# Dilated attention heads: tokens ordered by their rest by 4, 384 score columns per softmax row

## The chip, the cores and the metric

The kernel runs on one core of a Trainium2 chip, as one program from its inputs in DRAM to its output. The metric is the device time of one execution in microseconds (us); the tables give the median of several runs. The profile is of one execution of its own.

## The reference, cut to what matters

256 tokens of width 1024 go through two blocks of two layers each. The change lies in the second block, whose layers (`hybrid_layer`) have three branches: a short convolution, a latent attention and the dilated attention. In the dilated branch 8 heads of 64 look at the tokens in three groups, each with its own q, k and v:

```python
DIL_PATTERNS = ((128, 1), (512, 4), (2048, 16))   # window, dilation
for gi, (window, dilation) in enumerate(DIL_PATTERNS):
    o_g, lse_g = dilated_group_attention(dq[:, :, gi], dk[:, :, gi], dv[:, :, gi], slopes[gi],
                                         dilation, window // dilation)
alpha = jax.nn.softmax(jnp.stack(lses, axis=0), axis=0)
o_c = jnp.sum(alpha[..., None] * jnp.stack(outs, axis=0), axis=0)
```

Group 0 looks back over up to 128 tokens one by one. Group 1 looks at tokens a multiple of 4 back, group 2 at tokens a multiple of 16 back, causally, each with a bias that falls with the distance. So in groups 1 and 2 a token sees only tokens with its own rest by 4. The last two lines make one softmax of the three groups: a row of scores over all three, one maximum, one sum.

## The kernel before, in words

**Weights.** A load on SyncE's DMA queue (SP) brings 1 MB of weights into a tile `raw` (L328, two buffers and now and then a third). ScalarE (ACT) casts each half to `whi` (L350), VectorE (DVE) forms the rest `wlo` (L351). Each plain matmul of 512 columns (`mm`, L280) takes one of these against the activations `hT`. `tr` (L284) transposes a 128×128 block on TensorE (PE).

**Order.** On PE the order is written out: jobs are Python generators that say after how many microseconds they want to go on (`yield D_DQ`, `yield D_SOFTD`), and each emitted matmul moves the planner's clock by the time written beside it. The other engines' queues are ordered by the framework's scheduler, which looks at the program and at when inputs are expected.

**The dilated branch.** `dilated()` projects q, k and v in nine blocks of four units (one unit: a pair of heads, one of q, k, v, one group; 128 columns), for two token tiles t of 128. The epilogue `epi` normalizes q and k (`rows`, L1495), transposes them and copies them to `dq` (ACT, L1510) and `dk` (DVE, L1512). v units are copied from PSUM by ACT to `dvn` (L1500, two buffers) and moved by SP's DMAs to `dv` (L1502; all three tiles are called `dqkv` in the profile), since there the tokens change partitions. Each v run has two DMAs per token tile, of 64 rows and of 1 to 3 units of 512 bytes. Tokens are ordered by their rest by 2: the even ones are one tile, the odd ones the other. For comparison with these DMAs: L1307 loads `gc`, 64 rows of 4 bytes, and L629 loads `acc`, one row of 4 KB, both on SP too.

**One pair.** `dil_pair()` runs once a pair of heads (4 pairs in each of 2 layers), when the blocks with its q, k and v are done. It loads two bias tables `dtab` (L1532), then for each tile t and head (rows 0 to 63 or 64 to 127 of the array) makes four score matmuls of 128×128: two for group 0 (own tile and the other), one each for groups 1 and 2 (own tile: even distances contain the multiples of 4 and 16, the table masks the rest). DVE adds the table and takes the maximum (L1549), ACT takes exp with the sum (L1552), DVE the reciprocal (L1553), ACT scales the row (L1554): all on 128×512, called `dsm`. After D_SOFTD the four blocks of each `dsm` are transposed on PE and copied by ACT to `daT` (L1560), and 16 matmuls with 64 columns of `dv` as weights (PV) collect the output, which ACT copies to `ocT` (L1568).

Of the kernel before, what the change touches and what calls it, by code (L numbers as in the profile page):

```python
# [10 lines left out]
F32 = mybir.dt.float32  # L11
F32R = mybir.dt.float32r
AF = mybir.ActivationFunctionType
ALU = mybir.AluOpType
# [7 lines left out]
NEG = -1e30  # L22
BIG = 1e30
WB = 8
AT0, DSM, DAT, GT = 8, 4, 4, 2
# [114 lines left out]
def constants():  # L140
    f = np.float32
    o = {}
    i = np.arange(128)
# [25 lines left out]
    n = 24  # L169
    m = 2.0 ** (-8.0 * np.arange(1, n + 1) / n).reshape(3, 8)  # L170


    tab = np.zeros((8, 128, 5, 128))
    for c, (gi, off) in enumerate(((0, -1), (0, 0), (1, 0), (2, 0), (0, 1))):
        dl = (1, 4, 16)[gi]
        dist = 2 * (i[:, None] - i[None, :]) + off
        ok = (dist >= 0) & (dist % dl == 0) & (dist // dl <= 128)
        for h in range(8):
            tab[h, :, c] = np.where(ok, -m[gi, h] * dist * 8.0, NEG)
    o["k_dil"] = tab.reshape(8, 128, 640).astype(f)  # L180
    return o


# [49 lines left out]

DIL_COLS = [[(0, 1), (0, 0), (1, 0), (2, 0)], [(0, 1), (1, 1), (2, 1), (0, 0)]]


class Job:
# [6 lines left out]
class Kern:  # L246
# [1216 lines left out]
    def dilated(self, q, gqk, ocT):  # L1463
        V, A, wk = self.V, self.A, self.wk
        pj, jobs, bufs = [], {}, {}
        eo = lambda x, g, n, t: x.rearrange("p g (r t i) -> p g t r i", r=2, t=2)[:, g:g + n, t]

        def buf(p, s):
            if (p, s) not in bufs:
                bufs[p, s] = q.tile([128, 2, 384] if s == 2 else [128, 3, 256], F32, tag=("dq", "dk", "dv")[s], bufs=2,  # L1470
                                    name=self.nm("dqkv"))
            return bufs[p, s]

        def epi(b, t, _, ps):
# [29 lines left out]
            tp = self.trs(rows, nu).rearrange("p g (i r) -> p g r i", r=2)  # L1504
            for i, (p, s), g, n in runs:
                if s == 2:
                    continue
                part = tp[:, i - u0:i - u0 + n]
                if s == 0:
                    A.copy(eo(buf(p, 0), g, n, t), part)  # L1510
                else:
                    V.tensor_tensor(eo(buf(p, 1), g, n, t), part,  # L1512
                                    gqk[:, g:g + n, None, None].to_broadcast([128, n, 2, 64]), ALU.mult)
# [10 lines left out]
    def dil_pair(self, pr, dq, dk, dv, ocT, deps):  # L1524
# [3 lines left out]
        V, A = self.V, self.A  # L1528
        tabs = []
        for j in range(2):  # L1530
            tab = self.ph.tile([128, 640], F32, tag="dtab", bufs=2, name=self.nm("dtab"))
# [6 lines left out]
        for t in range(2):  # L1538
            for o in (0, 64):
                ps[t, o] = self.bank()  # L1540
            for i, (g, k) in enumerate(DIL_COLS[t]):
                for o in (0, 64):
                    self.mm(ps[t, o][:, i * 128:i * 128 + 128], dq[o:o + 64, g, t * 128:t * 128 + 128],
                            dk[o:o + 64, g, k * 128:k * 128 + 128], us=0.12)
        for t in range(2):
            for o in (0, 64):
                st = self.wk.tile([128, 6], F32, tag="st", bufs=8, name=self.nm("dst"))
                sm = self.ph.tile([128, 512], F32, tag="dsm", bufs=DSM, name=self.nm("dsm"))
                V.tensor_tensor_reduce(sm, ps[t, o], tabs[o // 64][:, t * 128:t * 128 + 512], 1.0, NEG, ALU.add, ALU.max,  # L1549
                                       st[:, 0:1])  # L1550
                V.tensor_scalar_mul(st[:, 2:3], st[:, 0:1], -0.125)
                A.activation(sm, sm, AF.Exp, bias=st[:, 2:3], scale=0.125, accum_out=st[:, 3:4])  # L1552
                V.reciprocal(st[:, 3:4], st[:, 3:4])  # L1553
                A.activation(sm, sm, AF.Copy, scale=st[:, 3:4])  # L1554
                sms[t, o] = sm
        yield D_SOFTD
        for t in range(2):
            for o in (0, 64):
                aTs[t, o] = self.ph.tile([128, 4, 128], F32, tag="daT", bufs=DAT, name=self.nm("daT"))
# [8 lines left out]
        A.copy(ocT[:, pr].rearrange("p (n r) -> p r n", r=2), pv[:, :256].rearrange("p (r n) -> p r n", r=2))  # L1568


def build(tc, a, stop=99):
# [66 lines left out]
```

## Time and profile before

| what | value |
|---|---|
| median of 3 runs | 1474.86 us (1474.18 to 1477.39) |
| the profiled execution, its own time | 1475.15 us |
| its span | 1473.2 us |
| PE, DVE, ACT busy, share of the span | 98%, 73%, 56% |
| dilated stretch of layer 0, of layer 1 | 880 to 1030 us, 1240 to 1390 us |

The span is what the profiler saw between the first and the last instruction; 1.95 us of the execution lie outside it. Lines of the timeline give the start, the length and the operation, with the output tile, the inputs and the shape; neighbours of one kind are drawn together with their count. Matmul records overlap, so their pace is the difference of starts. A matmul in 32-bit floats (scores, PV) has two records, a transpose or a plain matmul has one. On SP the length is that of the issue, not of the transfer. A window's line gives its ends and length, then the busy time of PE, of PE's weight loads, of DVE, ACT and POOL, each with its instructions, then the granted clock of PE, the DMA share and the GB/s.

### The profile page before, as it was taken

The page shows a single profiled execution, that of the slowest core. Times are in us where ns is not written, and L with a number is a line of the kernel's source. Part 1 is how long each engine was busy: PE and PEld are TensorE (multiplying, and loading weights), DVE is VectorE, ACT ScalarE, POOL GpSimd, SP SyncE. Part 2 cuts the span into 40 slices and gives each one's busy share as a digit, 9 for nine tenths or more (in the row PEclk, how much of TensorE's full clock was granted, in tenths as well). Part 3 has the DMA queues.
Part 4 walks back from the last instruction along what each step waited for, and adds up shares of the span by engine and source line. Part 5 has one row for each costly group of instructions (what it writes and reads, how often), then busy time and mean ns, then how long its engine had stood idle before and what let it go on. Part 6 is the DMA issues. An engine that isn't in the chain of part 4 may idle for free. (4 is left out here: it accounts for less than half of the span.)

```text
span 1473.2 us, 20311 instructions
## 1 busy us (share of the span) xinstructions
PE 1448.1 (98%) x7636; PEld 1193.5 (81%) x7636; DVE 1070.6 (73%) x1779; ACT 817.7 (56%) x1417; POOL 109.9 (7%) x88
## 2 busy tenths in 40 slices
PE   9999999999999999999999999999999999999998
PEld 6776788888887888888878788888888888888887
DVE  5698898956999848866378766666767976665674
ACT  4657556634534535665265754667445675566651
POOL 0000100000001100000022003120001101221000
PEclk9999999999999999999999999999999999999999
DMA  9757587765867638745444355544545535554542
GB/s 380 281 200 272 200 318 282 286 215 179 304 246 269 235 138 273 270 172 202 159 145 172 116 207 211 185 167 159 198 163 200 203 116 206 200 178 173 186 178 79
DMA packets 53093, 306.53 MB, mean 208 GB/s; under 512 B 7674, under 2 KB 12154, under 8 KB 20100
## 3 DMA queue, kind: packets, MB, share of 16 engines
q1 hardware_dynamic: 51988, 304.74, 57.5%
q8 instruction: 60, 0.98, 0.3%
q10 hardware_dynamic: 1008, 0.50, 0.1%
q14 instruction: 37, 0.30, 0.1%
HBM read 301.03 MB, written 1.05 MB: 205 GB/s over the span
## 5 line engine op out<-in xcount | busy, mean ns | idle before, releaser
L351 DVE TENSOR_TENSOR wlo<-raw,whi 128x1024 fp32r<-128x1024 f32 x448 | 533.9, 1214 | 128.5 <-ACT whi L350 126.9
L350 ACT CAST whi<-raw 128x1024 fp32r<-128x1024 f32 x450 | 458.7, 1044 | 235.9 <-PE p L280 176.9
L280 PE MATMUL p<-whi,hT 128*128 128x512 f32 (+1 forms) x1728 | 573.7, 400 | 1.1 <-ACT whi L350 0.5
L280 PEld LDWEIGHTS p<-whi,hT 128*128 128x128 f32 x1728 | 325.4, 189 | 74.3 <-issue 6.9
L280 PE MATMUL p<-hT,whi 128*128 128x512 f32 x1088 | 382.9, 402 | 0.0
L280 PE MATMUL p<-wlo,hT 128*128 128x512 f32 (+1 forms) x864 | 337.3, 390 | 1.5 <-DVE wlo L351 1.5
L280 PE MATMUL p<-hT,wlo 128*128 128x256 f32 x1088 | 286.5, 283 | 0.0
L280 PEld LDWEIGHTS p<-hT,whi 128*128 128x128 f32 x1088 | 198.0, 190 | 37.8 <-issue 0.7
L280 PEld LDWEIGHTS p<-hT,wlo 128*128 128x128 f32 x1088 | 206.9, 190 | 12.3
L280 PEld LDWEIGHTS p<-wlo,hT 128*128 128x128 f32 x864 | 163.5, 189 | 34.0 <-DVE wlo L351 2.7
L637 DVE SCALAR_TENSOR_TENSOR acc<-raw,csc,acc 128x1024 f32<-128x1024 f32 x80 | 102.2, 1278 | 4.4 <-DMA raw<-in_ada_w_dram 4.0
L514 POOL TENSOR_TENSOR dss<-dss,mh 128x8 f32<-128x8 f32 (+3 forms) x36 | 56.1, 1560 | 328.0 <-DVE dss L513 328.0
L280 PE MATMUL p<-whi,ah 128*128 128x512 f32 x176 | 69.7, 396 | 0.0
L280 PE MATMUL p<-whi,al 128*128 128x512 f32 x176 | 69.5, 395 | 0.0
L280 PE MATMUL p<-wlo,ah 128*128 128x512 f32 x176 | 69.5, 395 | 0.0
L1495 DVE TENSOR_TENSOR rows<-p,dss 128x512 f32<-128x512 f32 (+3 forms) x36 | 18.5, 514 | 46.2 <-POOL dss L514 46.2
L1018 ACT COPY fT<-p 128x256 f32<-128x256 f32 x72 | 26.1, 368 | 42.7 <-PE p L280 42.5
L280 PE MATMUL p<-whi,s 128*128 128x512 f32 x128 | 41.3, 397 | 0.0
L280 PEld LDWEIGHTS p<-whi,al 128*128 128x128 f32 x176 | 33.0, 187 | 8.1
L280 PEld LDWEIGHTS p<-wlo,ah 128*128 128x128 f32 x176 | 33.0, 187 | 7.9
L280 PEld LDWEIGHTS p<-whi,ah 128*128 128x128 f32 x176 | 33.0, 187 | 7.9
L280 PE MATMUL p<-whi,yh 128*128 128x512 f32 x96 | 38.4, 400 | 0.0
(278 smaller groups left out, 1628.3 us busy)
## 6 DMA issues: line engine op xcount, KB each, us to landing
raw<-in_w_in_dram SPq DMA_DIRECT2D x84, 1024.0 KB, 4.9
raw<-in_w_gu_dram SPq DMA_DIRECT2D x44, 1024.0 KB, 5.3
raw<-in_ada_w_dram SPq DMA_DIRECT2D x40, 1024.0 KB, 5.3
raw<-in_w_ret_dram SPq DMA_DIRECT2D x24, 1024.0 KB, 6.0
raw<-in_w_dn_dram SPq DMA_DIRECT2D x22, 1024.0 KB, 4.9
raw<-in_w_qkv_dram SPq DMA_DIRECT2D x11, 1024.0 KB, 10.0
as<-in_ada_s_dram SPq DMA_DIRECT2D x16, 512.0 KB, 8.8
raw<-in_w_ro_dram SPq DMA_DIRECT2D x8, 1024.0 KB, 5.2
```

Of the source, the lines that this page charges most:

```text
L280: self.T.matmul(out, lhsT=lhsT, rhs=rhs, start=first, stop=last, skip_group_check=skip)
L350: for ins in (self.A.copy(hi[:, :m * n], src), self.sub.tensor_tensor(lo[:, :m * n], src, hi[:, :m * n].bitcast(F32), ALU.subtract)):
L351: self.sub.tensor_tensor(lo[:, :m * n], src, hi[:, :m * n].bitcast(F32), ALU.subtract)):
L514: self.G.tensor_tensor(ss, ss, self.mh[:, :n], ALU.pow)
L637: self.V.scalar_tensor_tensor(acc, r[:, j * D:j * D + D], self.sc[:, k:k + 1], acc, ALU.mult, ALU.add)
L1018: A.copy(f, ps[:, 256:512])
L1495: V.tensor_tensor(d3(rows[:, :nu * 128]), d3(src), ss[:, :2 * nu, None].to_broadcast([128, 2 * nu, 64]), ALU.mult)
```

## The change

Tokens are ordered by their rest by 4: tile t holds the tokens with rests 2t and 2t+1, 64 each. A group 1 or 2 score block of one rest is now 64×64, and both groups' blocks share one block of 128 columns. A softmax row has 384 columns: two blocks for group 0, one for groups 1 and 2.

- Scores: 16 matmuls of 128×128 become 8 of 128×128 and 16 of 64×64.
- Transposes: 16 become 12. `dsm`, `daT` and the operations on them have 384 columns, the table 512 where it had 640.
- PV: 16 matmuls of 64×128 become 8 of 64×128 and 8 of 64×64.
- `dv` has six blocks of 128 columns: 0 and 1 for group 0, four (one a rest) for groups 1 and 2, whose keys share the 128 rows. The DMAs per token tile and v run were 2 (64 rows) and are 4 times the run's units (32 rows of 512 bytes): 24 a layer before, 96 after.

```diff
-DIL_COLS = [[(0, 1), (0, 0), (1, 0), (2, 0)], [(0, 1), (1, 1), (2, 1), (0, 0)]]
+DIL_COLS = [[1, 0, None], [1, None, 0]]
...
-        eo = lambda x, g, n, t: x.rearrange("p g (r t i) -> p g t r i", r=2, t=2)[:, g:g + n, t]
+        eo = lambda x, g, n, t: x.rearrange("p g (r t i) -> p g t r i", r=4, t=2)[:, g:g + n, t]
...
-                bufs[p, s] = q.tile([128, 2, 384] if s == 2 else [128, 3, 256], F32, tag=("dq", "dk", "dv")[s], bufs=2,
+                bufs[p, s] = q.tile([128, 6, 128] if s == 2 else [128, 3, 256], F32, tag=("dq", "dk", "dv")[s], bufs=2,
...
-                    for r in range(2):
-                        self.nc.sync.dma_start(buf(p, 2)[64 * t:64 * t + 64, r, cs(g, n)], nat[r:128:2, :n * 128])
+                    for r in range(4):
+                        for u in range(n):
+                            at, c = (64 * (r % 2), r // 2) if g + u == 0 else (64 * (g + u - 1), 2 + r)
+                            self.nc.sync.dma_start(buf(p, 2)[at + 32 * t:at + 32 * t + 32, c], nat[r:128:4, cs(u, 1)])
...
-            for i, (g, k) in enumerate(DIL_COLS[t]):
-                for o in (0, 64):
-                    self.mm(ps[t, o][:, i * 128:i * 128 + 128], dq[o:o + 64, g, t * 128:t * 128 + 128],
-                            dk[o:o + 64, g, k * 128:k * 128 + 128], us=0.12)
+            for i, k in enumerate(DIL_COLS[t]):
+                if k is not None:
+                    for o in (0, 64):
+                        self.mm(ps[t, o][:, i * 128:i * 128 + 128], dq[o:o + 64, 0, t * 128:t * 128 + 128],
+                                dk[o:o + 64, 0, k * 128:k * 128 + 128], us=0.12)
+                    continue
+                for g in (1, 2):
+                    for c in range(2):
+                        for o in (0, 64):
+                            at = t * 128 + c * 64
+                            self.mm(ps[t, o][c * 64:c * 64 + 64, i * 128 + g * 64 - 64:i * 128 + g * 64],
+                                    dq[o:o + 64, g, at:at + 64], dk[o:o + 64, g, at:at + 64], us=0.06)
...
-                sm = self.ph.tile([128, 512], F32, tag="dsm", bufs=DSM, name=self.nm("dsm"))
+                sm = self.ph.tile([128, 384], F32, tag="dsm", bufs=DSM, name=self.nm("dsm"))
...
-                A.copy(aTs[t, o], self.trs(sms[t, o], 4))
+                A.copy(aTs[t, o], self.trs(sms[t, o], 3))
...
-            for i, (g, k) in enumerate(DIL_COLS[t]):
-                for o in (0, 64):
-                    self.mm(pv[o:o + 64, t * 128:t * 128 + 128], dv[:, k, g * 128 + o:g * 128 + o + 64],
-                            aTs[t, o][:, i], t == 0 and i == 0, i == 3, 0.109, True)
+            order = sorted(enumerate(DIL_COLS[t]), key=lambda e: e[1] is None)
+            for j, (i, k) in enumerate(order):
+                for c in range(1 if k is not None else 2):
+                    n = 128 if k is not None else 64
+                    for o in (0, 64):
+                        self.mm(pv[o:o + 64, t * 128 + c * 64:t * 128 + c * 64 + n],
+                                dv[:, k if k is not None else 2 + 2 * t + c, o:o + 64],
+                                aTs[t, o][:, i, c * 64:c * 64 + n], t == 0 and j == 0, j == 2, n * 0.00085, True)
```

The tables in DRAM and the last copy to `ocT` follow the new order of the tokens. The lines of the new kernel stand 8 to 24 further down (L280 is L288, L328 is L336, L350 is L358, L1502 is L1513, L1552 is L1571, L1554 is L1573).

How it stands in the queues. First PE, the scores of the first pair in layer 0, before (`p` is a PSUM bank, one for each tile t and head; the first operand is `dq`, the second `dk`; the shape is the output's):

```order
L280 MATMUL p_8171<-whi_8024,hT 128x512
L280 MATMUL p_8186<-dqkv_7905,dqkv_7903 128x128
L280 MATMUL p_8187<-dqkv_7905,dqkv_7903 128x128
L280 MATMUL p_8186<-dqkv_7905,dqkv_7903 128x128
L280 MATMUL p_8187<-dqkv_7905,dqkv_7903 128x128
L280 MATMUL p_8186<-dqkv_7905,dqkv_7903 128x128
L280 MATMUL p_8187<-dqkv_7905,dqkv_7903 128x128
```

and after:

```order
L288 MATMUL p_8191<-whi_8038,hT 128x512
L288 MATMUL p_8206<-dqkv_7911,dqkv_7909 128x128
L288 MATMUL p_8207<-dqkv_7911,dqkv_7909 128x128
L288 MATMUL p_8206<-dqkv_7911,dqkv_7909 128x128
L288 MATMUL p_8207<-dqkv_7911,dqkv_7909 128x128
L288 MATMUL p_8206<-dqkv_7911,dqkv_7909 64x64
L288 MATMUL p_8207<-dqkv_7911,dqkv_7909 64x64
L288 MATMUL p_8206<-dqkv_7911,dqkv_7909 64x64
L288 MATMUL p_8207<-dqkv_7911,dqkv_7909 64x64
```

Before, all 16 had one shape. Now the first tile has four of 128×128 and eight of 64×64, the second two, eight and two: four changes of shape inside the scores. In the last pair of a layer, 36 plain matmuls of 512 columns now lie between the last projection block's end and the first transposes of `dsm`, where there were 30.

Second SP at the last block of layer 0, whose v run has three units, before:

```order
L1532 DMA dtab_8953<-in_k_dil_dram 128x640
L1532 DMA dtab_8955<-in_k_dil_dram 128x640
L1502 DMA dqkv_8866<-dvn_8864 64x384 x2
L328 DMA raw_9065<-in_w_in_dram 128x2048
L1502 DMA dqkv_8866<-dvn_8943 64x384 x2
L328 DMA raw_9131<-in_w_in_dram 128x2048
L328 DMA raw_9202<-in_w_out_b_dram 128x2048
```

and after:

```order
L1543 DMA dtab_9039<-in_k_dil_dram 128x512
L1543 DMA dtab_9041<-in_k_dil_dram 128x512
L336 DMA raw_9001<-in_w_in_dram 128x2048
L1513 DMA dqkv_8934<-dvn_8932 32x128 x12
L1513 DMA dqkv_8934<-dvn_9019 32x128 x12
L336 DMA raw_9149<-in_w_in_dram 128x2048
L336 DMA raw_9223<-in_w_in_dram 128x2048
L336 DMA raw_9293<-in_w_out_b_dram 128x2048
```

The weight load that stood between the two token tiles' DMAs (raw_9065, now raw_9149) stands behind both.

Third ACT at the softmax of the last pair in layer 0, before (the four `dsm` are the tile t and head rows; 9098 is the first):

```order
L1220 COPY z_9048<-p_9013 128x256
L350 CAST whi_9067<-raw_9065 128x1024
L1227 ACTIVATE z_9048<-z_9048 128x256
L350 CAST whi_9071<-raw_9065 128x1024
L350 CAST whi_9133<-raw_9131 128x1024
L1552 ACTIVATE dsm_9098,dst_9097<-dsm_9098,dst_9097 128x512
L1552 ACTIVATE dsm_9105,dst_9104<-dsm_9105,dst_9104 128x512
L1552 ACTIVATE dsm_9112,dst_9111<-dsm_9112,dst_9111 128x512
L1554 ACTIVATE dsm_9098<-dsm_9098,dst_9097 128x512
```

and after (9196 is the first):

```order
L1235 ACTIVATE z_9132<-z_9132 128x256
L358 CAST whi_9151<-raw_9149 128x1024
L358 CAST whi_9155<-raw_9149 128x1024
L1228 COPY z_9233<-p_9137 128x256
L358 CAST whi_9225<-raw_9223 128x1024
L358 CAST whi_9229<-raw_9223 128x1024
L1571 ACTIVATE dsm_9196,dst_9195<-dsm_9196,dst_9195 128x384
L1571 ACTIVATE dsm_9203,dst_9202<-dsm_9203,dst_9202 128x384
L1571 ACTIVATE dsm_9210,dst_9209<-dsm_9210,dst_9209 128x384
L1573 ACTIVATE dsm_9196<-dsm_9196,dst_9195 128x384
```

Three casts stood ahead of the first exponential and now there are four and a copy. Earlier in that queue, the copy of the last block's first tile to `dvn` has one more cast ahead of it.

## Rows read from the trace of the kernel before

**Rows 1.** The page: busy time by engine; the chain that ended last.

```profile
PE 1448.1 (98%) x7636; PEld 1193.5 (81%) x7636; DVE 1070.6 (73%) x1779; ACT 817.7 (56%) x1417; POOL 109.9 (7%) x88
...
PE 42%; DVE 3%; POOL 1%; issue 1%; ACT 1%; DMA 1%; DVEq 0%; POOLq 0%; ACTq 0%
```

**Rows 2.** Windows of the dilated stretches, both layers: busy us by engine, clock, DMA.

```profile
880.00:1030.00 150.00, 150.00 (x911) 124.35 (x911) 95.18 (x186) 93.50 (x165) 26.43 (x17) 1.00 0.51 178
1240.00:1390.00 150.00, 150.00 (x912) 124.34 (x911) 95.19 (x185) 93.47 (x165) 26.44 (x17) 1.00 0.52 178
```

**Rows 3.** PE timeline round the scores, first pair: start, us, operation, count.

```profile
917.65 0.40 PE L280 MATMUL p<-whi,hT 128*128 128x512 f32 x1
917.97 2.06 PE L280 MATMUL p<-dqkv,dqkv 64*128 64x128 f32 x32
919.96 0.50 PE L280 MATMUL p<-whi,hT 128*128 128x512 f32 x1
920.29 0.39 PE L280 MATMUL p<-wlo,hT 128*128 128x512 f32 x1
```

**Rows 4.** PE timeline round the PV matmuls, first pair.

```profile
941.08 0.39 PE L280 MATMUL p<-whi,hT 128*128 128x512 f32 x1
941.40 1.97 PE L280 MATMUL p<-daT,dqkv 128*64 128x128 f32 x32
943.30 0.44 PE L284 MATMUL p<-ident,rows 128*128 128x128 f32 x2
```

**Rows 5.** PE timeline round the softmax transposes, first pair.

```profile
927.94 0.49 PE L284 MATMUL p<-ident,rows 128*128 128x128 f32 x3
928.27 0.60 PE L284 MATMUL p<-ident,dsm 128*128 128x128 f32 x4
928.62 0.47 PE L280 MATMUL p<-whi,hT 128*128 128x512 f32 x1
```

**Rows 6.** SP timeline, last block of layer 0: start, us of issue, DMA, count.

```profile
987.89 1.11 SPq L1502 DMA_DIRECT2D dqkv<-dvn  x2
991.23 0.33 SPq L328 DMA_DIRECT2D raw<-in_w_in_dram  x1
994.76 1.10 SPq L1502 DMA_DIRECT2D dqkv<-dvn  x2
995.96 0.54 SPq L328 DMA_DIRECT2D raw<-in_w_in_dram  x1
```

**Rows 7.** Tile dqkv: ns of one operation, shortest, median, longest.

```profile
L1502 SPq DMA_DIRECT2D dqkv<-dvn x48: 464/551/883, 889.9 to 1354.2; - x48
...
L1510 ACT COPY dqkv<-p x24: 243/373/497, 889.7 to 1350.0; 128x384 f32<-128x384 f32 x8, 128x256 f32<-128x256 f32 x8, 128x128 f32<-128x128 f32 x8
```

**Rows 8.** Tiles gc and acc, DMAs of 64 and of one row.

```profile
L1307 SPq DMA_DIRECT2D gc<-in_mlag_dram x4: 516/586/596, 759.5 to 1121.7; - x4
...
L629 SPq DMA_DIRECT2D acc<-in_ada_b_dram x10: 243/244/322, 58.7 to 500.3; - x10
```

**Rows 9.** DMA issues: count, KB each, median us from issue to landing.

```profile
raw<-in_w_in_dram SPq DMA_DIRECT2D x84, 1024.0 KB, 4.9
```

**Rows 10.** ACT timeline, last pair of layer 0.

```profile
1001.31 1.05 ACT L350 CAST whi<-raw 128x1024 fp32r<-128x1024 f32 x1
...
1005.02 1.05 ACT L350 CAST whi<-raw 128x1024 fp32r<-128x1024 f32 x1 [1.41 <-PE p L280]
1006.41 0.72 ACT L1552 ACTIVATE dsm<-dsm,dst 128x512 f32<-128x512 f32 x1 [0.34 <-DVE dst L1551]
...
1008.96 1.95 ACT L1554 ACTIVATE dsm<-dsm,dst 128x512 f32<-128x512 f32 x3 [0.32 <-DVE dst L1553]
```

**Rows 11.** PE timeline ahead of the last pair's transposes, layer 0.

```profile
1012.24 0.40 PE L280 MATMUL p<-whi,hT 128*128 128x512 f32 x1
1012.47 0.60 PE L284 MATMUL p<-ident,dsm 128*128 128x128 f32 x4
```

More of the change, by code (lines that the diff above doesn't have):

```diff
@@ L170, in constants, with block @@
     m = 2.0 ** (-8.0 * np.arange(1, n + 1) / n).reshape(3, 8)
-    tab = np.zeros((8, 128, 5, 128))
-    for c, (gi, off) in enumerate(((0, -1), (0, 0), (1, 0), (2, 0), (0, 1))):
+    j = np.arange(128)
+    n_of = lambda tile, pos: 4 * (pos % 64) + 2 * tile + pos // 64
+    tab = np.zeros((8, 128, 4, 128))
+    def block(h, c, gi, dist):
         dl = (1, 4, 16)[gi]
-        dist = 2 * (i[:, None] - i[None, :]) + off
         ok = (dist >= 0) & (dist % dl == 0) & (dist // dl <= 128)
-        for h in range(8):
-            tab[h, :, c] = np.where(ok, -m[gi, h] * dist * 8.0, NEG)
-    o["k_dil"] = tab.reshape(8, 128, 640).astype(f)
+        return np.where(ok, -m[gi, h] * dist * 8.0, NEG)
+    own = 4 * (i[:, None] % 64 - i[None, :64])
+    for h in range(8):
+        for c, (tq, tk) in ((0, (0, 1)), (1, (0, 0)), (3, (1, 0))):
+            tab[h, :, c] = block(h, c, 0, n_of(tq, i)[:, None] - n_of(tk, j)[None, :])
+        tab[h, :, 2] = np.concatenate([block(h, 2, 1, own), block(h, 2, 2, own)], axis=1)
+    o["k_dil"] = tab.reshape(8, 128, 512).astype(f)
     return o
@@ L1500, in epi @@
                     A.copy(nat[:, :n * 128], ps[:, cs(i, n)])
-                    for r in range(2):
-                        self.nc.sync.dma_start(buf(p, 2)[64 * t:64 * t + 64, r, cs(g, n)], nat[r:128:2, :n * 128])
+                    for r in range(4):
+                        for u in range(n):
+                            at, c = (64 * (r % 2), r // 2) if g + u == 0 else (64 * (g + u - 1), 2 + r)
+                            self.nc.sync.dma_start(buf(p, 2)[at + 32 * t:at + 32 * t + 32, c], nat[r:128:4, cs(u, 1)])
             yield D_DQ
-            tp = self.trs(rows, nu).rearrange("p g (i r) -> p g r i", r=2)
+            tp = self.trs(rows, nu).rearrange("p g (i r) -> p g r i", r=4)
             for i, (p, s), g, n in runs:
@@ L1512, in epi @@
                     V.tensor_tensor(eo(buf(p, 1), g, n, t), part,
-                                    gqk[:, g:g + n, None, None].to_broadcast([128, n, 2, 64]), ALU.mult)
+                                    gqk[:, g:g + n, None, None].to_broadcast([128, n, 4, 32]), ALU.mult)
         for b in range(9):
@@ L1530, in dil_pair @@
         for j in range(2):
-            tab = self.ph.tile([128, 640], F32, tag="dtab", bufs=2, name=self.nm("dtab"))
+            tab = self.ph.tile([128, 512], F32, tag="dtab", bufs=2, name=self.nm("dtab"))
             self.nc.sync.dma_start(tab, self.a["k_dil"][2 * pr + j])
@@ L1558, in dil_pair @@
             for o in (0, 64):
-                aTs[t, o] = self.ph.tile([128, 4, 128], F32, tag="daT", bufs=DAT, name=self.nm("daT"))
-                A.copy(aTs[t, o], self.trs(sms[t, o], 4))
+                aTs[t, o] = self.ph.tile([128, 3, 128], F32, tag="daT", bufs=DAT, name=self.nm("daT"))
+                A.copy(aTs[t, o], self.trs(sms[t, o], 3))
                 yield D_SOFTD2
@@ L1563, in dil_pair @@
         for t in range(2):
-            for i, (g, k) in enumerate(DIL_COLS[t]):
-                for o in (0, 64):
-                    self.mm(pv[o:o + 64, t * 128:t * 128 + 128], dv[:, k, g * 128 + o:g * 128 + o + 64],
-                            aTs[t, o][:, i], t == 0 and i == 0, i == 3, 0.109, True)
-        A.copy(ocT[:, pr].rearrange("p (n r) -> p r n", r=2), pv[:, :256].rearrange("p (r n) -> p r n", r=2))
+            order = sorted(enumerate(DIL_COLS[t]), key=lambda e: e[1] is None)
[6 more added lines that the diff above has]
+                                aTs[t, o][:, i, c * 64:c * 64 + n], t == 0 and j == 0, j == 2, n * 0.00085, True)
+        A.copy(ocT[:, pr].rearrange("p (n r) -> p r n", r=4), pv[:, :256].rearrange("p (r n) -> p r n", r=4))
 def build(tc, a, stop=99):
```

2 lines of the change are left out of this document (1 added, 1 removed).

## The prediction

> **What bounds the kernel now.** I read the page first: TensorE (PE) is busy for 98% of the span and heads the chain of work that ended last [rows 1]. The change touches the dilated branch of the two hybrid layers, so I then read the busy time of those two stretches alone: in both, PE is busy for all of 150 us at full granted clock, while DVE and ACT stand near 95 and 93 [rows 2]. There PE is the bound and never waits. Two consequences: every PE pass that goes or comes changes the time one for one; and work saved on DVE or ACT is worth nothing by itself, but work that makes PE wait is paid in full. Then I read the PE timeline of one head pair (scores, transposes, PV), for the price of each piece [rows 3 to 5], and last SyncE's queue (SP), ACT and PE around the last pair of a layer, since the change multiplies SP's DMAs there [rows 6 to 11]. There are four pairs in each of two layers, so 8 pair runs.
>
> **PE work.** Records of matmuls overlap, so I go by start to start.
>
> Transposes: three of 128 columns take 928.27 − 927.94 = .33 us, .11 each [rows 5]. Four of 16 go per pair: −.44. This is the sure part, 3.5 us over 8 pairs.
>
> PV: 16 matmuls lie between 941.08 and 943.30, that is 2.22 less .23 for the plain matmul ahead (1012.24 to 1012.47 shows its pace [rows 11]), 1.99 us [rows 4]. Two records stand for each matmul (x32), so 32 passes of .11 would be 3.5 us: the two heads of a pair, which fill different column halves of the array, go side by side, in 16 steps of about .11, with some .2 at the ends. Now 8 of the 16 steps have 64 columns. Halved, they save 8 × .055 = .44; I take −.42. The other end is 0, if a step is held by its weight load, which the change doesn't shorten.
>
> Scores: from 917.65 to 920.29 is 2.64, less two plain matmuls of .23, 2.18 us for 16 scores [rows 3]. Again two heads go side by side (here in different row halves), 16 steps of about .11 = 1.79, and .4 is left for the ends: the first score starts .32 after a plain matmul that takes .23, so .09 is lost at the entry, its first steps lose another .1, and .33 to the next plain start shows another .09 at the exit. Now there are 8 scores of 128 columns (8 steps, .9) and 16 of 64×64, which can stand four in the array: four sets of two passes of 64 columns, .057 each, .46. If each change of tile shape costs what the ends show, about .2 into 64×128 and .14 into 64×64, the four changes inside (two of each kind) cost .68. So .9 + .46 + .68 + .4 = 2.44, against 2.19: **+.25 per pair**. Bounds: without any loss inside 1.76, −.42 — I keep −.32 for it, since the first steps of a set lose something; with two tiles at a time rather than four, the sets cost .92, +.7. I take the middle because the rows show a loss at every entry and exit of a small shape.
>
> The Trainium skill, "TensorEngine Tiling (Array Packing)", Key Properties, says "Changing tiling mode (not just tile) drains the TensorE"; by that rule, with which the .09 at each end agrees, the sum stays as above, and without it the scores come to the lower bound, the third rival below.
>
> Sum: −.44 − .42 + .25 = −.61 per pair, **−4.9 us** over 8 (bounds −9.4 and, with all dear ends, about +2).
>
> **Work beside PE.** ACT's and DVE's rows of 384 columns rather than 512 (a 128-column step is .13 us by the copies of 128, 256 and 384 [rows 7]) shorten work that PE doesn't wait for [rows 2]: nothing by themselves. The table load of 256 rather than 320 KB, and copies with finer strides: nothing, the same cover. It would cost something only where these are late, which is the next term.
>
> **SP's DMAs.** V leaves `dvn` by DMA: 24 per layer before, 96 now, with the same bytes. At the last block of a layer two per token tile become 12. They stand in SP's queue ahead of the weight loads, and the order now puts the load that stood between the tiles behind all 24. Before, that load was issued at 991.23 and the next at 995.96, with two DMAs at 987.89 and two at 994.76 [rows 6]. Behind it hang ACT's casts of these weights, and behind four of them (three before) and a copy, in ACT's queue, the exponentials and scales of the last pair, and behind these PE's transposes. The weights themselves are needed far later; it is the softmax that is caught.
>
> Price of one DMA issue, start to start, r: a 64-row one takes .47 to .59 us, whatever its width [rows 7], with .05 between: two in a row take 1.11, and the second is a dear one. None in the trace has 32 rows. From the side of few rows: a one-row DMA takes .24 to .32, a 64-row one of 4 bytes .52 to .60 [rows 8]; a straight line from .30 to .59 gives .445 + .05 = .49 for 32 rows. If rows don't matter, .59 + .05 = .64 in a long burst. The cheapest bound is the lone weight load, .33 + .05 = .38 [rows 6]. I take **r = .57**, between .49 and .64.
>
> Then: the first tile's copy stands behind one more cast (1.05, [rows 10]), so its burst starts about 988.9 and ends 988.9 + 12 × .57 = 995.7; the second starts then (its data is there at 994.76 [rows 6]) and ends 1002.6. The load lands 4.9 later [rows 9], 1007.5. From the start of the first cast to the first scaled row it took 1001.31 to about 1009.66 before (the three scales start at 1008.96, .7 for the first [rows 10]), 8.35; three narrower exponentials take .13 each off: 8.0 (7.5 to 8.4). Ready: 1015.5. PE wanted it at 1012.47 [rows 11]; by the new order six more plain matmuls stand ahead (+1.36), while about three transposes (−.33) and one PV (−.42) of the pair before and this pair's scores (+.25) move it to 1013.3. So PE, which had 2.8 us to spare, waits **2.2 us**, and in both layers, whose stretches repeat each other [rows 2], **4.4**. What is late next is the other transposes, spaced wider than ACT's scales, so nothing is added. Of the other blocks' bursts (4 or 8 DMAs per tile) I count nothing: they are shorter and eat spare time.
>
> Sum: −4.9 + 4.4 = −.5 us against the profiled run's 1475.15 (span 1473.2 and 1.95 around it). That run lies .29 above the median shown, so I predict **1474.5**: no change that can be told. What a measurement of this kernel can tell is about 0.2%, 2.9 us.
>
> **Rivals.**
> - *Cheap issue.* If r is .47 or less, the burst ends at 1000.4, the rows are ready at 1013.3, and PE never waits: −4.9, **1470**. For it: fewer rows, and the first DMA of a pair takes .47 [rows 7]. Against: the second takes .59, and 11 of 12 are not first.
> - *Dear bursts; the other side.* SP's issue is the one mechanism: from r = .64 on, the wait (3.9 per layer) outweighs what PE saves by 2.9 us; at .70 ready is 1018.6, the wait 5.3, in all +5.7, **1480.5**. For it: 64 rows cost more than the load's 128, so rows don't set the price, and a burst of 12 can pile up where a pair doesn't. Against: no row shows a pile.
> - *No loss inside the scores.* PE saves 9.4, but the last pair is due .57 earlier, so the wait is 2.75 per layer: −9.4 + 5.5, **1471**; with cheap issue 1466.
> - *The small score tiles go two at a time.* PE saves 1.3, the wait shrinks to 1.75 per layer: +2.2, **1477**. PV steps, whose column halves run side by side with their weight loads hidden [rows 4], speak against it. The Trainium skill, "TensorE: Matmul & The Clock Gate", Part 3 (What overlaps and what doesn't), has a weight load overlap running matmuls only when its row group differs; that would give this rival for the two column tiles of one row group, and the PV rows disagree.
>
> **How the numbers follow.** Forecast (r .49 to .64, losses inside) .30, from −4.4 to +2.8; cheap issue .25; dear bursts .22; no loss inside .15; two at a time .08. Faster by over 0.2%: .25 + .11 + .05 = .41. Slower: .21 + .03 + .01 = .25. Within: .34. The range leaves out the cheap end of the third rival and bursts above r = .71: 1466 to 1481.5. Cases of both signs hold most of the chance; the forecast's own range is 1470 to 1477.5.
>
> **What would show it.** In the profile after: 12 transposes per pair and PV near 1.6 us from start to start; scores near 2.4 (1.8 for the third rival, 2.9 for the fourth); on SP, bursts of 12 with r to be read directly; the next weight load near 1002.6 less what PE saved before; and on PE a gap of about 2 us ahead of the last pair's transposes in both layers, put down to the scale on ACT. No gap and 1470: cheap issue. A gap above 4: dear bursts. Wrong altogether would be gaps at other pairs, or PE waiting for `dv` itself.

## The result, and the profile after

| kernel | median us | against the kernel before |
|---|---|---|
| before | 1473.93 | |
| after | 1484.16 (1480.91 to 1485.34, 6 runs) | ratio 1.0067 (1.0055 to 1.0079): 9.9 us slower |

The profiled execution took 1482.21 us, its span is 1480.4. The page's chain, by engine (compare [rows 1]):

```profile
PE 31%; DVE 6%; DMA 4%; ACT 3%; issue 2%; POOL 1%; SPq 1%; POOLq 0%; ACTq 0%; DVEq 0%
```

PE holds 31% of the chain where it held 42%; DVE, DMA and ACT have come in. So somewhere another engine now ends last. The list of waits (who waited for whom; us in total, times, longest) says where, in its first row for PE:

```profile
PE p L292 <- ACT dsm L1573: 10.6, 4, 4.4
```

No such row stands in the profile of before: the transposes of `dsm` wait for ACT's scale, four times. The windows of [rows 2] again, now of the changed kernel:

```profile
880.00:1030.00 150.00, 145.06 (x934) 118.07 (x934) 89.94 (x184) 86.28 (x161) 22.82 (x17) 0.99 0.50 176
1240.00:1390.00 150.00, 144.36 (x907) 117.47 (x906) 90.91 (x183) 85.50 (x160) 22.83 (x17) 0.98 0.48 169
```

PE, busy for all of 150 us before, has 4.94 and 5.64 us idle, 10.6 together, and the granted clock is no longer 1.00.

**PE's own work** came out near the forecast. The PE timeline round the scores, PV and one group of transposes (compare [rows 3 to 5]):

```profile
914.58 0.40 PE L288 MATMUL p<-whi,hT 128*128 128x512 f32 x1
914.91 2.34 PE L288 MATMUL p<-dqkv,dqkv 64*128 64x128 f32 x48
...
917.52 0.39 PE L288 MATMUL p<-wlo,hT 128*128 128x512 f32 x1
...
937.84 0.39 PE L288 MATMUL p<-whi,hT 128*128 128x512 f32 x1
938.16 1.56 PE L288 MATMUL p<-daT,dqkv 128*64 128x128 f32 x32
939.65 0.44 PE L292 MATMUL p<-ident,rows 128*128 128x128 f32 x2
...
1019.44 0.49 PE L292 MATMUL p<-ident,dsm 128*128 128x128 f32 x3
1019.69 0.48 PE L288 MATMUL p<-whi,hT 128*128 128x512 f32 x1
```

Scores: 917.52 − 914.58 = 2.94, less two plain matmuls of .23, 2.48 us (2.18 before). PV: 939.65 − 937.84, less .23, 1.58 (1.99 before). Three transposes take .25 where four took .35, four times a pair. So +.30 − .41 − .40 = −.51 a pair, **−4.1 us** over 8 pairs.

**SP's queue.** The second burst of the seventh block and the ninth block of layer 0 (compare [rows 6]), and the row of the DMAs (compare [rows 7]):

```profile
965.52 7.64 SPq L1513 DMA_DIRECT2D dqkv<-dvn  x12
973.26 1.00 SPq L336 DMA_DIRECT2D raw<-in_w_in_dram  x2
...
986.59 15.62 SPq L1513 DMA_DIRECT2D dqkv<-dvn  x24
1002.30 1.00 SPq L336 DMA_DIRECT2D raw<-in_w_in_dram  x2
```

```profile
L1513 SPq DMA_DIRECT2D dqkv<-dvn x192: 467/592/1548, 886.8 to 1365.1; - x192
```

A burst of 12 takes 7.64, so .636 us from issue to issue; the 24 of the ninth block take 15.62, and 16.07 in layer 1, where a single issue takes 1.55. A DMA of 32 rows costs SP what one of 64 rows cost as the second of a pair, .59 and a gap of .05. The weight load that was issued at 991.23 goes out at 1002.30. From its issue to its landing such a load takes 4.9 us in the median, as before [rows 9], so the load is late because it is issued late.

**ACT behind it**, then **PE**, last pair of layer 0 (compare [rows 10, 11]). In the second group the first two rows are the third pair's, and the last row is layer 1's last pair:

```profile
1007.39 2.00 ACT L358 CAST whi<-raw 128x1024 fp32r<-128x1024 f32 x2 [8.61 <-DMA raw<-in_w_in_dram]
1009.30 0.36 ACT L1228 COPY z<-p 128x256 f32<-128x256 f32 x1
1009.81 2.00 ACT L358 CAST whi<-raw 128x1024 fp32r<-128x1024 f32 x2 [0.15 <-DMA raw<-in_w_in_dram]
1011.88 0.61 ACT L1571 ACTIVATE dsm<-dsm,dst 128x384 f32<-128x384 f32 x1
...
1014.16 1.12 ACT L1573 ACTIVATE dsm<-dsm,dst 128x384 f32<-128x384 f32 x2 [0.38 <-DVE dst L1572]
```

```profile
980.95 0.39 PE L288 MATMUL p<-whi,hT 128*128 128x512 f32 x1
982.43 0.55 PE L292 MATMUL p<-ident,dsm 128*128 128x128 f32 x3 [1.08 <-ACT dsm L1573]
...
1010.59 0.39 PE L288 MATMUL p<-whi,hT 128*128 128x512 f32 x1
1014.83 0.90 PE L292 MATMUL p<-ident,dsm 128*128 128x128 f32 x3 [3.86 <-ACT dsm L1573]
1015.38 0.78 PE L288 MATMUL p<-whi,hT 128*128 128x512 f32 x1
1015.96 0.63 PE L288 MATMUL p<-wlo,hT 128*128 128x512 f32 x1
...
1378.46 0.90 PE L292 MATMUL p<-ident,dsm 128*128 128x128 f32 x3 [4.45 <-ACT dsm L1573]
```

The casts wait for the load (8.61 us idle on ACT), the exponentials stand behind four casts and a copy, the first scaled row is there at 1014.8, and PE, which had come to it at 1010.8 (.23 after its last plain matmul), waits 3.86 us; in layer 1 4.45. At the third pair it waits 1.08 (1.19 in layer 1). The brackets give the wait and its releaser.

**The clock.** Windows of 4 us round the two long waits (PE busy in column 2, granted clock third from the end):

```profile
1012.00:1016.00 4.00, 1.17 (x5) 1.07 (x6) 4.00 (x14) 3.62 (x11) 0.00 (x0) 0.83 0.61 238
1016.00:1020.00 4.00, 4.00 (x16) 3.21 (x15) 3.39 (x6) 4.00 (x8) 0.00 (x0) 0.74 0.76 262
1020.00:1024.00 4.00, 4.00 (x20) 3.29 (x19) 4.00 (x4) 3.58 (x5) 0.00 (x0) 1.00 0.19 33
...
1376.00:1380.00 4.00, 1.54 (x5) 1.36 (x6) 4.00 (x13) 3.62 (x12) 0.00 (x0) 0.56 0.54 229
1380.00:1384.00 4.00, 4.00 (x13) 3.13 (x12) 3.39 (x5) 4.00 (x8) 0.00 (x0) 0.59 0.74 262
```

After the long waits the granted clock is .74 to .83 in these windows in layer 0 and .56 to .59 in layer 1: PE is at the lower level (1.2 GHz) for about 3.4 us in layer 0 and 6.8 in layer 1, the end of the wait included; plain matmuls start .42 or more apart (1015.96 − 1015.38 = .58 at the first, where an entry is in it) and not .23. After the short waits at the third pair it stays 1.00. Busy time weighted with what is missing to 1.00 gives 1.17 × .17 + 4 × .26 = 1.2 us and 1.54 × .44 + 4 × .41 = 2.3 us. Added up in stretches of 2 us, it is 1.4 and 2.4, **3.8 us**.

So −4.1 of PE's work, +10.6 of waits, +3.8 of clock: +10.3, where the runs show +9.9. The spans of the two profiled executions differ by 7.2 only, since this one came to the first scores at 914.58 and that of before at 917.65 [rows 3], 3.1 earlier, ahead of all changed work on PE. Of these 3.1, 1.9 are clock: counted in the same way, the lower level cost 7.9 us ahead of 880 us in the execution before and 5.9 in this one. So the 3.8 are read from the two dilated stretches, where the clock stays at 1.00 before; over the whole span, the two profiled executions differ by only 1.8 in clock. Executions of one kernel differ by as much.

### The profile page after: what moved, and what is told of

Its sections match the earlier page's. It is cut to its first block, busy times and chain, and to the rows that moved or that the text cites. A ratio compares the mean times of both kernels' runs of the same rounds, so it can differ in the third digit from the quotient of the medians.

```text
span 1480.4 us, 20715 instructions
## 1 busy us (share of the span) xinstructions
PE 1445.4 (98%) x7732; PEld 1187.0 (80%) x7732; DVE 1066.0 (72%) x1779; ACT 811.0 (55%) x1417; POOL 102.8 (7%) x88
## 5 line engine op out<-in xcount | busy, mean ns | idle before, releaser
L358 ACT CAST whi<-raw 128x1024 fp32r<-128x1024 f32 x450 | 458.4, 1044 | 268.9 <-PE p L288 175.5
L288 PE MATMUL p<-whi,hT 128*128 128x512 f32 (+1 forms) x1728 | 576.0, 401 | 0.6 <-DVE hT L527 0.4
L288 PEld LDWEIGHTS p<-whi,hT 128*128 128x128 f32 x1728 | 326.8, 190 | 73.8 <-issue 7.0
L288 PE MATMUL p<-hT,whi 128*128 128x512 f32 x1088 | 382.4, 402 | 0.0
L288 PE MATMUL p<-wlo,hT 128*128 128x512 f32 (+1 forms) x864 | 338.5, 392 | 0.1
L288 PE MATMUL p<-hT,wlo 128*128 128x256 f32 x1088 | 286.2, 283 | 0.0
L288 PEld LDWEIGHTS p<-hT,whi 128*128 128x128 f32 x1088 | 197.8, 189 | 37.4 <-issue 0.3
L288 PEld LDWEIGHTS p<-hT,wlo 128*128 128x128 f32 x1088 | 206.7, 190 | 12.2
L288 PEld LDWEIGHTS p<-wlo,hT 128*128 128x128 f32 x864 | 164.2, 190 | 32.3 <-issue 1.9
L522 POOL TENSOR_TENSOR dss<-dss,mh 128x8 f32<-128x8 f32 (+3 forms) x36 | 48.9, 1359 | 335.4 <-DVE dss L521 335.4
L288 PE MATMUL p<-whi,ah 128*128 128x512 f32 x176 | 69.7, 396 | 0.0
L288 PE MATMUL p<-whi,al 128*128 128x512 f32 x176 | 69.5, 395 | 0.0
L288 PE MATMUL p<-wlo,ah 128*128 128x512 f32 x176 | 69.5, 395 | 0.0
L288 PE MATMUL p<-whi,s 128*128 128x512 f32 x128 | 41.3, 397 | 0.0
L288 PEld LDWEIGHTS p<-whi,al 128*128 128x128 f32 x176 | 33.0, 187 | 8.0
L288 PEld LDWEIGHTS p<-wlo,ah 128*128 128x128 f32 x176 | 33.0, 187 | 8.0
L288 PEld LDWEIGHTS p<-whi,ah 128*128 128x128 f32 x176 | 33.0, 188 | 7.9
L1027 DVE TENSOR_TENSOR fT<-p,fT 128x256 f32<-128x256 f32 x72 | 28.7, 418 | 14.4 <-ACT fT L1026 14.2
```

The lines of the kernel that those rows point to most:

```text
L288: self.T.matmul(out, lhsT=lhsT, rhs=rhs, start=first, stop=last, skip_group_check=skip)
L358: for ins in (self.A.copy(hi[:, :m * n], src), self.sub.tensor_tensor(lo[:, :m * n], src, hi[:, :m * n].bitcast(F32), ALU.subtract)):
L522: self.G.tensor_tensor(ss, ss, self.mh[:, :n], ALU.pow)
L1027: V.tensor_tensor(f, ps[:, 0:256], f, ALU.add)
```

## Experiments

Each was timed beside the kernel before on its chip. "By the profile" is PE's work as above, plus idle time of PE in the two dilated stretches, plus the clock's part.

| kernel | ratio to before (95%) | us against before | by the profile |
|---|---|---|---|
| after | 1.0067 (1.0055 to 1.0079) | +9.9 | −4.1 + 10.6 + 3.8 = +10.3 |
| two DMAs | .9976 (.9963 to .9988) | −3.5 | −4.1 |
| before, DMAs cut | 1.0132 (1.0115 to 1.0150) | +19.4 | 12.2 + 3.0 = +15.2 |
| two DMAs, scores sorted | .9945 (.9926 to .9964) | −8.1 | −8.7 |
| late DMAs | .9976 (.9965 to .9987) | −3.5 | −4.1 |
| late DMAs, scores sorted | **.9922 (.9908 to .9937)** | −11.5 | −8.7 |
| cut in the ninth block alone | 1.0006 (.9992 to 1.0019) | +.9 | −4.1 + 6.0 + 1.7 = +3.6 |
| cut in the seventh block alone | .9970 (.9954 to .9985) | −4.4 | −4.1 |
| cut in the seventh and ninth | 1.0040 (1.0024 to 1.0056) | +5.9 | −4.1 + 7.3 + 3.2 = +6.4 |
| cut in all but the ninth | .9988 (.9975 to 1.0000) | −1.8 | −4.1 + 2.4 = −1.7 |
| softmax first | 1.0050 (1.0035 to 1.0065) | +7.4 | −4.1 + 6.0 = +1.9 |

The clock's part comes from one profiled execution, which need not be a typical one. The mean granted clock of every execution is on record too, and its difference from the mean of the kernel before, times 1475 us, is an estimate of the time that the clock costs over the whole span. In place of the clock's part it gives 12.2 + 6.1 = +18.3 for the kernel before with its DMAs cut (mean clock .9904, before .9945), −8.7 − 1.5 = −10.2 for the late and sorted one (.9952, before .9942), −4.1 + 6.0 − .1 = +1.8 for the ninth block alone (.9942, as before) and −4.1 + 6.0 + 3.0 = +4.9 for softmax first (.9922, before .9942). All four come nearer to what was measured; where in these executions the clock fell is not on record.

**1. The DMAs alone put back.**

```diff
-                    for r in range(4):
-                        for u in range(n):
-                            at, c = (64 * (r % 2), r // 2) if g + u == 0 else (64 * (g + u - 1), 2 + r)
-                            self.nc.sync.dma_start(buf(p, 2)[at + 32 * t:at + 32 * t + 32, c], nat[r:128:4, cs(u, 1)])
+                    for r in range(2):
+                        self.nc.sync.dma_start(buf(p, 2)[64 * t:64 * t + 64, 3 * r + g:3 * r + g + n],
+                                               nat[r:128:2, :n * 128].rearrange("p (u c) -> p u c", c=128))
```

> The changed kernel with only the v transfers put back to 2 DMAs of 64 rows per token tile and v run (24 a layer); v rows then stand in the wrong places of dv, all else is as in the change. Theory A (SP's issues delay a weight load, and the casts that wait for it hold the last softmaxes on ACT): PE no longer waits for the scale at L1573, no stretch of lower granted clock, and what is left is PE's saving, .55 us a pair: 4.4 us faster than before, ratio .997. Rival B (the new PE work itself, small tiles and changes of shape, costs the time): still 5 to 10 us slower than before.

Measured: 1470.34 against 1473.30, 3.5 us faster by the ratio. The window of layer 0 (layer 1's reads the same, 150.00 and 1.00):

```profile
880.00:1030.00 150.00, 150.00 (x968) 122.70 (x967) 94.66 (x187) 91.06 (x166) 26.42 (x17) 1.00 0.52 181
```

PE is busy all the time again, at full clock. The whole loss, and more, hangs on V's DMAs; the rival that PE's new work costs the time is out.

**2. The DMAs alone added to the kernel before.**

```diff
                     for r in range(2):
-                        self.nc.sync.dma_start(buf(p, 2)[64 * t:64 * t + 64, r, cs(g, n)], nat[r:128:2, :n * 128])
+                        for h in (0, 64):
+                            for u in range(n):
+                                at = 64 * t + h // 2
+                                self.nc.sync.dma_start(buf(p, 2)[at:at + 32, r, cs(g + u, 1)],
+                                                       nat[h + r:h + 64:2, cs(u, 1)])
```

> The kernel before with only the v transfers cut into 32 rows and one unit each (96 a layer, the same result). Theory A: bursts of 12 at .64 us; the weight load behind the last burst is issued near 1004 us and lands near 1009, the last softmax is ready near 1013, PE waits about .6 us there and 1 to 2 us at the third pair: 2 to 6 us slower than before. Rival B: no change, since PE's work is that of before.

Measured: 1492.49 against 1473.30, +19.4. The sign was right, the size far over what was expected. The waits of PE in it:

```profile
989.71 1.11 PE L284 MATMUL p<-ident,dsm 128*128 128x128 f32 x4 [3.78 <-ACT dsm L1558]
...
1356.87 0.66 PE L284 MATMUL p<-ident,dsm 128*128 128x128 f32 x4 [4.44 <-ACT dsm L1558]
```

The largest wait is at the third pair (3.78 and 4.44, shown), not at the last (1.40 and .72, with .6 expected), and the second pair waits too (.79 and 1.07). At the third pair the seventh block's second burst stands ahead of the loads on SP:

```profile
969.58 7.88 SPq L1505 DMA_DIRECT2D dqkv<-dvn  x12
977.56 8.73 SPq L328 DMA_DIRECT2D raw<-in_w_in_dram  x3
```

With rows of 512 columns the softmax behind them is longer, too. The expectation looked at the ninth block and undersized the seventh, as the prediction had. About 4 us of the 19.4 are not in the sum by the profile, whose execution (1490.56) was 1.9 shorter than the median. By the mean clock of all its executions some 3 of them are clock; about 1 stays open.

**3. Scores sorted by shape** (on the kernel of experiment 1): the loop over the 64×64 tiles comes after that over the 128×128 blocks of both token tiles.

```diff
         for t in range(2):
             for i, k in enumerate(DIL_COLS[t]):
                 if k is not None:
                     for o in (0, 64):
                         self.mm(...)
-                    continue
-                for g in (1, 2):
+        for t in range(2):
+            i = DIL_COLS[t].index(None)
+            for g in (1, 2):
```

> As the run with the two DMAs (v rows in the wrong places), and the scores of a pair in two blocks, first the eight of 128x128, then the sixteen of 64x64: one change of shape inside where there were four. If a change costs .14 to .2 us as counted: .5 us less a pair, scores near 2.0 us in place of 2.5, 4 us faster than the run with the two DMAs, 8 faster than before. If it is the small passes that are slow: as the run with the two DMAs, within 1 us.

Measured: 1463.76 against 1473.30, and under experiment 1 by 6.6 (medians) or 4.6 (ratios in the table). PE's timeline:

```profile
918.12 0.40 PE L288 MATMUL p<-whi,hT 128*128 128x512 f32 x1
918.44 1.79 PE L288 MATMUL p<-dqkv,dqkv 64*128 64x128 f32 x48
...
920.49 0.40 PE L288 MATMUL p<-wlo,hT 128*128 128x512 f32 x1
```

920.49 − 918.12 less .46 is 1.91 us where the unsorted scores took 2.48: three changes of shape fewer are worth .57, .19 each, and 4.6 over 8 pairs, as the ratios have it. So the time inside the scores is that of the changes of shape, as the prediction took it from the ends of [rows 3]; the sixteen small tiles do go four at a time (.9 + .46 + one change of .19 + .4 at the ends is 1.95). The Trainium skill's rule in "TensorEngine Tiling (Array Packing)", Key Properties, is that a change of tiling mode drains TensorE; the .19 agree with it.

**4. The same DMAs, later in SP's queue.** The complete change with all its 96 DMAs a layer, but each burst is a job of its own that is written into the program 18 us of the planner's clock later, and `dvn` has four buffers.

```diff
-                    nat = q.tile([128, 384], F32, tag="dvn", bufs=2, name=self.nm("dvn"))
+                    nat = q.tile([128, 384], F32, tag="dvn", bufs=4, name=self.nm("dvn"))
...
-                    for r in range(4):
-                        for u in range(n):
-                            at, c = (64 * (r % 2), r // 2) if g + u == 0 else (64 * (g + u - 1), 2 + r)
-                            self.nc.sync.dma_start(buf(p, 2)[at + 32 * t:at + 32 * t + 32, c], nat[r:128:4, cs(u, 1)])
+                    self.spawn(to_dv(buf(p, 2), nat, g, n, t), DV_LATE)
```

> The changed kernel, complete, with all its 96 DMAs a layer, but each burst is written into the program 18 us later (dvn has 4 buffers for it), so that in SP's queue weight loads stand ahead of it: at the last block both loads stand between the two bursts. Theory A: the waits for the scale go, 4.4 us faster than before. If the issues as such cost the time, wherever they stand: as the changed kernel, 10 us slower. If the bursts now make PV late: a new wait of PE for dv's DMAs ahead of PV.

Measured: 1470.05 against 1473.30, 3.5 us faster. SP at the ninth block:

```profile
987.82 7.48 SPq L1487 DMA_DIRECT2D dqkv<-dvn  x12
995.39 1.00 SPq L337 DMA_DIRECT2D raw<-in_w_in_dram  x2
996.49 10.75 SPq L1487 DMA_DIRECT2D dqkv<-dvn  x12
```

Twelve issues still take 7.48 us, but both weight loads go out at 995.39, between the bursts. The number and the usual price of the issues are the same as in the changed kernel (.59 in the median; this second burst even takes 10.75); what is queued behind them differs. The four buffers are a second difference, but ACT's copies to `dvn` wait as little for a free buffer in the changed kernel (2.3 us in all) as here (2.0). The 18 us are a place in the program and not a delay: the ninth block's first burst starts at 987.82 (986.59 in the changed kernel) and its last issue ends at 1007.24 (1002.21). V is 1 to 5 us later there, and PE doesn't wait for it.

**5. Both mended.** Experiment 4 with the sorted scores of experiment 3.

> The complete changed kernel with its DMAs written 18 us later and the scores sorted by shape. If the two gains add (3.3 us for the late DMAs, 6.6 for the sorted scores, as measured one by one): 9 to 10 us faster than before. If the earlier scores and the later v rows meet in a new wait: less, with a row of PE waiting ahead of PV or of the transposes.

Measured: 1462.57 against 1473.78, ratio .9922, 11.5 us faster than before. It is the complete change, and it is faster than the kernel before and than the changed kernel. By the profile 8.7 us are explained, with the mean clock 10.2; PE has no idle time in the dilated stretches.

**6. Which bursts?** The cut DMAs in some blocks alone, the two old ones in the others:

```diff
+                    if b - B_DIL != 8:
+                        for r in range(2):
+                            self.nc.sync.dma_start(buf(p, 2)[64 * t:64 * t + 64, 3 * r + g:3 * r + g + n],
+                                                   nat[r:128:2, :n * 128].rearrange("p (u c) -> p u c", c=128))
+                    else:
```

and the cut ones under the `else`; with `!= 6`, `not in (6, 8)` and `== 8` in the other three.

> The changed kernel with its cut v transfers in the ninth block of each layer alone (48 DMAs over both layers in place of 192, 24 issues a layer there); the other blocks have 2 of 64 rows per token tile, and their v rows stand in the wrong places. Theory A: the 24 issues ahead of the weight load make the wait at the last pair alone, 4 us a layer, with the lower clock after it (1.5 us a layer); none at the third pair: 7 to 8 us slower than the run with the two DMAs, 4 to 5 slower than before. If the loss is spread over all bursts: a quarter of it, 3 us over the run with the two DMAs.

> The same, with the cut transfers in the seventh block of each layer alone (24 issues a layer, its v rows right, the others in the wrong places). Theory A: only the wait at the third pair, 1 to 1.3 us a layer, and the clock stays at its upper level, since a wait of that length did not lower it in the changed kernel: 2 to 2.5 us slower than the run with the two DMAs, still about 1 us faster than before. If a burst of 24 costs the same wherever it stands: as the run with the cut transfers in the ninth block.

> The changed kernel with the cut v transfers in the seventh and the ninth block of each layer (the others 2 of 64 rows, their v rows in the wrong places). Taken one by one, the seventh cost nothing over the run with the two DMAs and the ninth 3 to 4 us, while all together cost 13. If it is these two that add up (the third pair's burst leaves the last pair less spare time): waits of about 4 us at the last pair and up to 1 at the third, the lower clock in both layers, 7 to 10 us slower than before. If the earlier blocks' bursts are needed for it: as the run with the ninth block alone, equal to before within 2 us.

> The changed kernel with the cut v transfers in all blocks but the ninth. If the earlier bursts use up the third pair's spare time: waits of 1 to 1.3 us a layer at the third pair, none at the last, clock at its upper level: 1 to 2 us faster than before, 2 over the run with the two DMAs. If every burst's cost is only passed on to the last pair: no wait at all, as the run with the two DMAs.

Measured: +.9, −4.4, +5.9 and −1.8 us against before. PE's waits at `dsm` in the first (ninth block alone, both layers), the third (seventh and ninth) and the fourth (all but the ninth):

```profile
1012.47 0.55 PE L292 MATMUL p<-ident,dsm 128*128 128x128 f32 x3 [2.83 <-ACT dsm L1578]
...
1371.34 0.55 PE L292 MATMUL p<-ident,dsm 128*128 128x128 f32 x3 [3.13 <-ACT dsm L1578]
```

```profile
1015.69 0.55 PE L292 MATMUL p<-ident,dsm 128*128 128x128 f32 x3 [3.29 <-ACT dsm L1578]
...
1375.53 0.90 PE L292 MATMUL p<-ident,dsm 128*128 128x128 f32 x3 [3.99 <-ACT dsm L1578]
```

```profile
984.16 0.55 PE L292 MATMUL p<-ident,dsm 128*128 128x128 f32 x3 [0.89 <-ACT dsm L1578]
...
1340.57 0.55 PE L292 MATMUL p<-ident,dsm 128*128 128x128 f32 x3 [1.22 <-ACT dsm L1578]
```

Bursts don't add one by one. The seventh block's alone make no wait, the ninth's alone wait 2.83 and 3.13. With both, the last pair waits 3.29 and 3.99, and the third pair still not at all; with the earlier blocks' too, the last waits 3.86 and 4.45, and the third .89 to 1.22. So each burst first uses up time that PE had to spare, and what the bursts before it have used is gone: the ninth block's price rose by about 1.2 us a layer through the others. What they use can be seen where the ninth block's burst starts. With the ninth block's cut DMAs alone, in layer 0:

```profile
983.53 15.61 SPq L1518 DMA_DIRECT2D dqkv<-dvn  x24
...
1009.25 0.39 PE L288 MATMUL p<-whi,hT 128*128 128x512 f32 x1
```

PE comes to the transposes at 1009.48, 25.9 us after the first issue; in the changed kernel it is 24.2 (986.59 to 1010.8).

Three of the four expectations missed. For the ninth block alone 4 us a layer was the number of the full change, too much by 1, and +.9 came where 4 to 5 were expected; for the seventh alone a wait of 1 to 1.3 a layer was expected and none came; for both +5.9 came where 7 to 10 were expected. The run without the ninth came out as expected.

**7. Softmax first.** The five softmax operations of `dil_pair` inside `with self.first():`, a higher priority for the scheduler.

> The complete changed kernel with the softmax given a higher priority in the scheduler. All 96 DMAs a layer stay on SP. At the last pair two casts stand ahead of the exponentials where there were four, and these two read a weight load that now stands between the two bursts; at the third pair two more casts come between the exponentials. Theory A (it is the place of the casts in ACT's queue that makes PE wait): the wait at the last pair, 4 us a layer, and the lower clock there go; the wait at the third pair grows from 1.2 to 3 to 4 us a layer: 0 to 5 us slower than before, where the changed kernel is 10 slower. If the burst as such held PE: as the changed kernel.

Measured: 1482.43 against 1473.78, +7.4, outside the expected 0 to 5. The waits moved to where they were expected, PE waits for the scale at the third pair and no longer at the last one, but with 2.28 and 1.73 they are shorter than the 3 to 4 expected:

```profile
988.46 0.55 PE L292 MATMUL p<-ident,dsm 128*128 128x128 f32 x3 [2.28 <-ACT dsm L1574]
...
1348.63 0.55 PE L292 MATMUL p<-ident,dsm 128*128 128x128 f32 x3 [1.73 <-ACT dsm L1574]
```

```profile
961.06 15.46 SPq L1513 DMA_DIRECT2D dqkv<-dvn  x24
976.62 1.00 SPq L336 DMA_DIRECT2D raw<-in_w_in_dram  x2
...
1000.16 0.52 SPq L336 DMA_DIRECT2D raw<-in_w_in_dram  x1
```

The ninth block's first load stands between its bursts here (1000.16), the seventh block's two loads stand behind all 24 (976.62), and the wait is where the loads are behind. That bears the mechanism out. The time doesn't: idle PE in the dilated stretches is 6.0 us (4.0 here, 2.0 ahead of PV for `daT`, which was not expected) and the clock stays up there, which gives +1.9. The profiled execution (1478.61) was among the shortest of six, 3.8 under the median. Its mean clock was .993, the other short one's .994; three of the four longer ones had .991. So part of what these lost is clock (3.0 us over all six, by the estimate above); about 2.5 of the 7.4 stay open.

## Why the prediction was wrong

Right, step by step:

- What bounds the kernel, and that work on ACT and DVE is worth nothing by itself: with V's DMAs put back (experiment 1) PE is busy throughout, and 3.5 us were saved where PE's own saving is 4.1.
- PE's terms: −.44, −.42 and +.25 a pair were forecast, −.40, −.41 and +.30 came; −4.9 against −4.1 us. The middle that was taken for the scores, a loss at each change of shape, is what experiment 3 shows.
- The path of the loss: SP's issues, the load behind them, the casts, the softmax behind the casts, the transposes. Also the load's landing and the chain on ACT: from the first issue of the ninth block's burst to the first scaled row, 988.9 to 1015.5 was forecast with r = .57, and with r = .64 it is 28.3 us; measured 986.59 to 1014.76, 28.2. From the same issue to the point where PE comes to the transposes, 24.4 was forecast and 24.2 measured.

Wrong:

1. **The price of an issue, r.** The step "I take r = .57, between .49 and .64" leaned on a straight line from one row to 64 rows. Rows between 32 and 64 don't matter: .636 measured, the upper end. With the rest of the sum as it stood, that alone makes the wait at the last pair 3.9 us instead of 2.2; 3.86 and 4.45 were measured (the burst of layer 1 is .45 longer than that of layer 0). The rival "dear bursts; the other side" named this point, r = .64, and its price there, 2.9 us slower, but that is a third of what came.
2. **The other blocks.** "Of the other blocks' bursts (4 or 8 DMAs per tile) I count nothing" was wrong twice: the seventh block's v run has three units too, so 12 DMAs per tile, and with all bursts in place its softmax, the third pair's, waits 1.08 and 1.19. And bursts that make no wait take spare time from the next (experiment 6). Missed: 2.3 us at the third pair. The prediction had itself named "gaps at other pairs" as the sign that it is wrong altogether. At the last pair the other blocks' part, about 1.2 us a layer, was largely in the sum without being named: the prediction took the late start of the ninth block's burst from the order of the queues (one more cast ahead of the copy). So the 3.9 are right in size but are not the price of the ninth block's DMAs by themselves, which is 2.83 and 3.13.
3. **What a wait does to the clock.** No term for it. After the two long waits PE ran on at the lower level for a while, 3.8 us over both in the profiled execution.

With −4.1, 2 × 4.15, 2.3 and 3.8 the sum is +10.3. The range ended at 1481.5, because the dearest case took r = .71 with the last pair alone, and nothing stood in it for the second and third point. Two slips in the working change nothing: at r = .47 the burst ends at 1000.2 and not 1000.4, and the sum for the forecast is 1474.4 and not 1474.5.

## What to carry to other kernels

When an edit multiplies the DMAs on a queue, price each at what the second of two in a row costs there, not at the first or a smaller one, and ask what stands behind the burst and which engine's queue that in turn blocks: moving the same 96 DMAs so that weight loads go out between the bursts gave back the whole loss. Bursts use up the spare time of those behind them, so cost them together. And where small tiles of different shapes take turns on TensorE, sort them by shape.

## What the runs showed of the hardware that was not expected

- An issue on SP of these DMAs costs the same for 32 rows of 512 bytes and for 64 rows of 512 to 1536 bytes: .47 us as the first, .59 and a gap of .05 as the next (64 rows were seen in pairs only). Single ones in a burst took up to 1.55 us (`L1513`, longest).
- In the dilated stretches the granted clock fell to the lower level for about 3.4 and 6.8 us after waits of PE of 3.86 and 4.45 us; it fell as well after those of 3.13, 3.29 and 3.99 in experiment 6 and of 3.78 and 4.44 in experiment 2, and it did not after those of .72 to 2.83.
- A change between tiles of 64×128 and 64×64 costs about .19 us on TensorE (experiment 3, three changes fewer); four 64×64 tiles run side by side, as the sum of 1.95 against the measured 1.91 has it.

The waits in the second point are no rule by the length of a wait. Near 95 us every profiled execution has one and the same wait of PE, 3.37 or 3.38 us, for `rows`; the window behind it reads, in the kernel before and then in the run with the ninth block alone:

```profile
96.00:98.00 2.00, 2.00 (x8) 1.71 (x7) 1.75 (x3) 0.67 (x2) 0.20 (x1) 0.50 1.25 373
...
96.00:98.00 2.00, 2.00 (x13) 1.73 (x12) 1.91 (x5) 0.33 (x1) 0.96 (x1) 1.00 0.85 315
```

One fell to .50, the other stayed at 1.00. In the kernel before, the clock also fell, to .61 from 1174 to 1176 us, after two waits of only 1.52 and .66. What decides is not shown here.
